# Projecting attention's queries turned and unnormed, with row factors inside the scores' maximum

## The chip, the cores and the metric

The kernel runs on one core of one Trainium2 chip. A core has TensorE (PE, matrix products, with its weight loads shown apart as PEld), VectorE (DVE), ScalarE (ACT), GpSimd (POOL) and SyncE (SP, which here only issues DMAs). Each engine works through its own queue in order and waits on semaphores for the others. The metric is the device time of one execution in microseconds (us); the profile gives, for one such execution, the span from the first to the last instruction.

## The reference, cut to what matters

One encoder layer over two sequences of 512 tokens and width 1024: an S5 state-space branch and a windowed attention branch are gated, added and projected, and a squared-ReLU MLP follows. The change is in attention (16 query heads, 4 key/value heads, head width 64, blocks of 128 tokens, each seeing itself and its neighbours):

```python
h = rms_norm(x, ln1)
q, k, v, u, g_att, g_ssm = jnp.split(h @ w_in, IN_SPLITS, axis=-1)
q = rms_norm(q.reshape(bsz, seq_len, N_HEADS, HEAD_DIM), q_gain)   # per token and head
k = rms_norm(k.reshape(bsz, seq_len, N_KV_HEADS, HEAD_DIM), k_gain)
s = jnp.einsum('nqkgd,njkd->nkgqj', qb, kw) * HEAD_DIM ** -0.5 + bias
s = jnp.where(mask, s, NEG_INF)
p = jax.nn.softmax(jnp.concatenate([s, sink_col], axis=-1), axis=-1)[..., :-1]
o = jnp.einsum('nkgqj,njkd->nqkgd', p, vw)
```

`rms_norm(q)` divides each row (token and head) of the projected queries by the root of its mean square, and multiplies by a gain per column. The divisor is one number per token and head, so it may be applied before or after the product with the keys.

## The kernel before, in words

Products that need full precision are done in three: both operands are split into a high part, rounded by a cast on ACT, and a low rest, subtracted on DVE (or POOL), and high x high, high x low and low x high are added in PSUM.

**The first stage** (0 to some 220 us) projects `u` in eight columns of 128 and the gates in sixteen. The weights of each column come in two DMAs of 256 KB into `c_raw` tiles (two buffers), issued on SP by `column_in` (L212 to L219), are cast on ACT (L222) and split on DVE (L223). The finished columns are stored by SP (`u_store`, L173). Each engine's order is written out by hand here: `fill` holds PE's steps, `cast_owed`, `dve_owed` and `act_owed` what the other engines owe. Column 5 is asked for when column 3's last product is issued; on SP its two loads stand behind three stores of `u` that wait for DVE (L422).

**The attention stage** (436 to some 650 us) has eight steps, one for each key head `j` (0 to 3) and sequence `sq`: `steps = (0,0), (0,1), (1,0), ... (3,1)`. A step has four units `qb`, one for each block of 128 queries, and a unit has four heads. The order on PE, ACT, DVE and POOL is that of the program's text (a manual schedule), so that work of three units lies interleaved:

- the unit itself: `scores` (L1154, PE: high and low keys against the queries), `largest` (L1158, DVE: one custom operation that writes minus (score + bias) to `p` and the minimum to `nmx`), `exp` (L1164, ACT, with the row's sum);
- the unit before (`prev`): its `p` is transposed (L1170), split (L1174 ACT, L1179 DVE) and multiplied with the values (L1186);
- the queries of the next step (`Tile`, four in a step, one in each unit): `project` (L811: 24 products, 128 tokens of `hT` as weights, 256 columns of `w_q` moving), `square` (ACT, L1101), `power` (DVE row sums L1105, POOL L1107 and L1108: x^-0.5), `norm` (DVE, L1112), `turn` (PE, two transposes, L1117), `high` and `low` (two each of 64x256: ACT L1130, DVE L1134) into the tile `qa`.

Keys are copied twice side by side by POOL (`kd`, L1072), transposed (L1081) and split once a step, in the first unit. POOL also multiplies the step's result by its gate and by the softmax's divisors (L1232, L1235), makes the low parts of later query weights (L805), and puts the sink into `p` (L1146). The biases of a key head (128 x 384 for each of its four heads, five buffers) are loaded by SP (L1066) in the last unit before they are needed.

The core of `Tile` and of the maximum, before:

```python
def norm(self):
    self.qn = ap.tile([P, 2, G, HD], F32, tag="qn", name="qn")
    V.tensor_mul(self.qn[:, 0], self.psv, self.rq[:, :, None].to_broadcast([P, G, HD]))

def largest(self, h):
    V.tensor_tensor_reduce(self.p[:, h, 1:1 + self.nk], self.s[h][:, 0:self.nk],
                           biases[self.j][h][:, b0:b0 + self.nk], -1.0,
                           nsink[:, hh:hh + 1], ALU.add, ALU.min, self.nmx[:, h:h + 1])
```

Of the kernel before, what the change touches and what calls it, by code (L numbers as in the profile page):

```python
# [64 lines left out]
def hybrid_layer(ctx, tc, x, xT, rel, onehot, early, w_qkv, w_ug, q_gain, k_gain, sink,  # L65
# [46 lines left out]
    nsink = const.tile([P, N_HEADS], F32, name="nsink")  # L112

# [97 lines left out]

    def column_in(n):  # L212

        src = w_ug[U_BLK + n] if n < KT else w_ug[GA_BLK + n - KT]
        w = weights[n] = [cpool.tile([P, KT, P], F32R, tag=tag, name=tag) for tag in ("c_hi", "c_lo")]
        for i in range(2):
            sl = slice(i * KT // 2, (i + 1) * KT // 2)
            raw = cpool.tile([P, KT // 2, P], F32, tag="c_raw", name="c_raw")
            SP.dma_start(raw, src[:, sl, :])  # L219
# [54 lines left out]
    with tc.tile_pool(name="xin", bufs=2, reuse_waits="tile") as xin, tc.tile_pool(name="ssmc", bufs=1) as sc:  # L274
# [261 lines left out]
        for k in range(KT):  # L536
# [246 lines left out]
    class Block:  # L783
# [24 lines left out]
        def multiply(self, ps, act, col, i0, i1):  # L808
            for i in range(i0, min(i1, 3 * KT)):
                k, p = divmod(i, 3)  # L810
                PE.matmul(ps, act[p == 2][:, k, col:col + P], self.w[k // 4][p == 1][:, k % 4, :],  # L811
                          start=i == 0, stop=i == 3 * KT - 1)
# [240 lines left out]
    with tc.tile_pool(name="att", bufs=2, reuse_waits="tile") as ap:  # L1053
# [32 lines left out]
        class Tile:  # L1086


            def __init__(self, j, sq, t):
                self.key, self.t, self.k, self.qn = (j, sq), t, 0, None  # L1090
# [7 lines left out]
            def square(self):  # L1098
                self.psv = self.ps.rearrange("p (h d) -> p h d", h=G)
                self.sq = ap.tile([P, G, HD], F32, tag="sq", name="sq", bufs=1)  # L1100
                S.activation(self.sq, self.psv, AF.Square, scale=HD ** -0.5)  # L1101

            def power(self):
                ms = small.tile([P, G], F32, tag="ms", name="ms")
                V.reduce_sum(ms, self.sq, axis=AX.X)  # L1105
# [4 lines left out]
            def norm(self):  # L1110
                self.qn = ap.tile([P, 2, G, HD], F32, tag="qn", name="qn")
# [23 lines left out]

        class Unit:


            def __init__(self, j, sq, qb, sums, ya):
                self.j, self.sq, self.qb, self.sums, self.ya = j, sq, qb, sums, ya  # L1140
# [14 lines left out]

            def largest(self, h):
                hh, b0 = self.j * G + h, (self.k0 - self.qb + 1) * P
                V.tensor_tensor_reduce(self.p[:, h, 1:1 + self.nk], self.s[h][:, 0:self.nk],  # L1158
                                       biases[self.j][h][:, b0:b0 + self.nk], -1.0,
# [150 lines left out]
        prev = owed = lower = turned = None  # L1310
# [7 lines left out]
        if True:  # L1318
            rows = entry()
            for i, (j, sq) in enumerate(steps):  # L1320
# [11 lines left out]
                for qb in range(NB):  # L1332
# [7 lines left out]
                    cur = Unit(j, sq, qb, sums, ya)  # L1340
# [6 lines left out]
                    new = Tile(*nxt, qb) if nxt else None  # L1347
                    project = new.project if new else nop
                    kd = None
                    new_biases = (lambda h: load_biases(nxt[0], h)) if nxt and qb == NB - 1 and sq == 1 else nop  # L1350
                    new_biases(0)
                    cur.scores(0)
                    cur.largest(0)
                    new_biases(1)
# [33 lines left out]
                    if rows and not rows.qn:  # L1388
                        rows.norm()
# [835 lines left out]
```

## Time and profile before

| | us |
|---|---|
| Median of 3 runs (lowest, highest) | 1437.83 (1437.75, 1438.02) |
| The profiled execution's own time | 1437.74 |
| Its span | 1436.0 |
| PE, DVE, ACT, POOL busy in it | 1426.7, 1083.2, 770.0, 161.5 |
| Attention stage, first to last unit's start | 436.1 to 641.0 |

The page's rows name a line, an engine, an operation, what it writes and reads, shapes, a count, and then busy time, the mean length of one in ns, and idle time before them with what ended it. A timeline's rows begin with start and duration in us; rows of equal instructions that follow each other are merged (x4), and a bracket gives the idle time before and what ended it. A matmul's recorded length is longer than its share of the engine, since matmuls are pipelined; its cost is read from start to start. A row of a table of stretches gives the stretch, its length, and the busy time and count of PE, PEld, DVE, ACT and POOL, then the granted clock, the DMA engines' share and GB/s.

### The profile page before, as it was taken

To read this page: it belongs to the slowest core of one execution; us is meant where nothing else is said; L and a number is where in the kernel's file an instruction comes from. 1 tells how busy PE (TensorE), PEld (TensorE's weight loads), DVE (VectorE), ACT (ScalarE), POOL (GpSimd) and SP (SyncE) were. 2 spreads that over 40 slices of the span, in tenths; PEclk is the share of its full clock that TensorE was granted. 3 is DMA by queue.
4 is the path that set the end of the run, shared out by engine and by line. 5 is a ranking of instruction groups with operands and counts; after the bars stand their busy time and mean duration, and the time that the engine had idled before them with its cause. 6 is when DMAs were issued, how large, how long until landed. Compare 5 with 4: busy or idle time off the path is not lost.

```text
span 1436.0 us, 21706 instructions
## 1 busy us (share of the span) xinstructions
PE 1426.7 (99%) x7864; PEld 1220.5 (85%) x7864; DVE 1083.2 (75%) x1869; ACT 770.0 (54%) x1390; POOL 161.5 (11%) x230
## 2 busy tenths in 40 slices
PE   9999999999999999999999999999999999999998
PEld 7788888889999999988888888888888888888887
DVE  8799989984637999987754898777776598575644
ACT  7589862234428998895432455545544444333332
POOL 2000010000313554470001100000000000000000
PEclk9999999999999999999999999999999999999999
DMA  8546467358822443356752334444443984464341
GB/s 310 178 153 186 167 208 270 110 194 289 258 81 67 119 130 100 119 184 236 259 178 90 133 118 162 161 161 161 144 140 120 350 323 137 139 201 146 119 132 59
DMA packets 130823, 243.88 MB, mean 170 GB/s; under 512 B 15723, under 2 KB 58987, under 8 KB 130716
## 3 DMA queue, kind: packets, MB, share of 16 engines
q1 hardware_dynamic: 106428, 187.39, 41.0%
q10 hardware_dynamic: 21888, 46.15, 8.5%
q0 software_dynamic: 2400, 8.95, 1.9%
q8 instruction: 62, 1.02, 0.3%
q14 instruction: 45, 0.37, 0.1%
HBM read 174.25 MB, written 80.77 MB: 178 GB/s over the span
## 4 chain that ended last, share of the span: by engine, by line
PE 86%; DVE 7%; DMA 2%; ACT 2%; issue 1%; SPq 0%; POOL 0%; ACTq 0%; DVEq 0%
PE bank L117 14%; PE bank L116 14%; PE bank L118 14%; PE acc L811 9%; PE acc L142 6%; PE acc L849 5%; PE acc L116 3%; PE acc L118 3%; PE acc L117 3%; PE po L1186 3%; PE sps L1154 2%; PE tps L1170 2%; PE sps L956 2%; PE sps L683 2%; DVE tt L887 2%; DMA c_raw<-in_w_ug_dram 1%
## 5 line engine op out<-in xcount | busy, mean ns | idle before, releaser
L117 PE MATMUL bank<-b_lo,a_hi 128*128 128x512 f32 x440 | 171.4, 390 | 0.0
L118 PE MATMUL bank<-b_hi,a_lo 128*128 128x512 f32 x440 | 171.2, 389 | 0.0
L116 PE MATMUL bank<-b_hi,a_hi 128*128 128x512 f32 x440 | 171.2, 389 | 0.0
L2098 ACT CAST a_hi<-d_a 128x1024 fp32r<-128x1024 f32 x55 | 58.1, 1056 | 179.0 <-PE bank L117 175.5
L2099 DVE TENSOR_TENSOR a_lo<-d_a,a_hi 128x1024 fp32r<-128x1024 f32 x55 | 67.3, 1224 | 98.5 <-ACT a_hi L2098 96.4
L116 PE MATMUL bank<-act,u_hi 128*128 128x512 f32 x256 | 99.6, 389 | 0.0
L117 PE MATMUL bank<-act,u_hi 128*128 128x512 f32 x256 | 99.6, 389 | 0.0
L118 PE MATMUL bank<-act,u_lo 128*128 128x512 f32 x256 | 99.6, 389 | 0.0
L117 PEld LDWEIGHTS bank<-b_lo,a_hi 128*128 128x128 f32 x440 | 82.6, 188 | 17.7 <-DVE b_lo L2099 0.6
L116 PEld LDWEIGHTS bank<-b_hi,a_hi 128*128 128x128 f32 x440 | 82.6, 188 | 17.2
L118 PEld LDWEIGHTS bank<-b_hi,a_lo 128*128 128x128 f32 x440 | 82.6, 188 | 16.9
L811 PE MATMUL acc<-w_hi,hT 128*128 128x256 f32 x384 | 84.4, 293 | 0.0
L811 PE MATMUL acc<-w_hi,act 128*128 128x256 f32 x384 | 81.2, 290 | 0.0
L142 PE MATMUL acc<-act,c_hi 128*128 128x512 f32 x256 | 80.8, 395 | 0.0
L142 PE MATMUL acc<-hT,c_hi 128*128 128x512 f32 x256 | 80.8, 395 | 0.0
L1164 ACT ACTIVATE p<-p,nmx 128x257 f32<-128x257 f32 (+1 forms) x128 | 72.1, 564 | 13.0 <-DVE nmx L1158 12.3
L1158 DVE CUSTOM_DVE_ANT_0 p<-sps,bias,nsink 128x256 f32<-128x256 f32 (+1 forms) x128 | 69.3, 542 | 4.3 <-PE sps L1154 2.9
L1882 ACT CAST u_hi<-s 128x512 fp32r<-128x512 f32 x64 | 39.3, 622 | 59.0 <-PE bank L117 40.3
L2099 DVE TENSOR_TENSOR b_lo<-k,b_hi 128x1024 fp32r<-128x1024 f32 x55 | 67.0, 1219 | 0.0
L811 PEld LDWEIGHTS acc<-w_hi,hT 128*128 128x128 f32 x384 | 63.8, 190 | 0.9
L811 PEld LDWEIGHTS acc<-w_hi,act 128*128 128x128 f32 x384 | 63.1, 190 | 0.8
L1179 DVE TENSOR_TENSOR pl<-tps,ph 128x512 fp32r<-128x512 f32 x80 | 55.0, 687 | 4.5 <-ACT ph L1174 2.7
(417 smaller groups left out, 3906.9 us busy)
## 6 DMA issues: line engine op xcount, KB each, us to landing
d_a<-a_scr SPq DMA_DIRECT2D x55, 512.0 KB
u_raw<-in_w_up_dram SPq DMA_DIRECT2D x32, 512.0 KB
a_scr<-t ACTq DMA_DIRECT2D x64, 256.0 KB
k<-in_w_down_dram SPq DMA_DIRECT2D x32, 512.0 KB
a_scr<-a ACTq DMA_DIRECT2D x48, 256.0 KB
c_raw<-in_w_ug_dram SPq DMA_DIRECT2D x44, 256.0 KB
u_sb<-u_scr SPq DMA_DIRECT2D x64, 128.0 KB
ct_scr<-ctab SPq DMA_DIRECT2D x16, 512.0 KB
```

Source lines behind the costliest of these rows:

```text
L116: PE.matmul(ps, a[0], b[0], start=first, stop=False)
L117: PE.matmul(ps, a[0], b[1], start=False, stop=False)
L118: PE.matmul(ps, a[1], b[0], start=False, stop=last)
L142: PE.matmul(self.ps[s], self.w[p == 2][:, k, :], hT[s][p == 1][:, k, :], start=i % (3 * KT) == 0, stop=i % (3 * KT) == 3 * KT - 1)
L811: PE.matmul(ps, act[p == 2][:, k, col:col + P], self.w[k // 4][p == 1][:, k % 4, :], start=i == 0, stop=i == 3 * KT - 1)
L849: PE.matmul(self.ps[s], w_g[self.m][p == 2][:, k, :], y_part(s, int(p == 1), k), start=k + p == 0, stop=k == KT - 1 and p == 2)
L1158: V.tensor_tensor_reduce(self.p[:, h, 1:1 + self.nk], self.s[h][:, 0:self.nk], biases[self.j][h][:, b0:b0 + self.nk], -1.0, nsink[:, hh:hh ...
L1164: S.activation(p, p, AF.Exp, bias=self.nmx[:, h:h + 1], scale=-1.0, accum_out=self.sums[:, h, self.qb:self.qb + 1])
L1179: V.tensor_sub(pl, self.pt[i], self.hl[i][0].bitcast(F32))
L1186: PE.matmul(self.po, vv, self.hl[i][part], start=i + part == 0, stop=i == self.nkb - 1 and part == 1)
L2098: S.copy(hi, src)
L2099: V.tensor_sub(lo, src, hi.bitcast(F32))
```

## The change

In six of the eight steps (`steps[1:-1]`) the queries come as two `Pair`s of heads instead of four `Tile`s. The weights of two heads (128 columns) are now the stationary operand and 512 tokens of `hT` move, so the product comes out turned (head dimensions on partitions), and needs no transposes; it is split at once, with the gain but without the norm. ACT squares it, and PE multiplies the squares (as weights, 128 tokens at a time) with `pair_ones`, a 128x2 matrix of ones in its two halves, which gives each token's sum of squares for both heads. DVE adds EPS, and POOL makes `minus` = -1/rms and `root` = rms from it. POOL then writes bias x rms into `p` for the unit that comes next (`prepare`), and `largest` reads it from there, with `minus` in place of -1: -(1/rms) x (score + bias x rms) is what stood there before. The pairs' 48 products a step are issued as a stream, five of them ahead. The biases' loads are all issued before the unit's first score. In the first stage, the raw weights of column 5 are asked for some 10 us of program order sooner, ahead of the stores.

```diff
+    pair_ones = const.tile([P, 2], F32, name="pair_ones")
...
+    def column_raws(n):
+        src = w_ug[U_BLK + n] if n < KT else w_ug[GA_BLK + n - KT]
+        raws_in[n] = []
+        for i in range(2):
+            raw = cpool.tile([P, KT // 2, P], F32, tag="c_raw", name="c_raw")
+            SP.dma_start(raw, src[:, i * KT // 2:(i + 1) * KT // 2, :])
...
+            if k == 3:
+                column_raws(5)
...
+        def multiply_turned(self, ps, act, m, i0, i1):
+            for i in range(i0, i1):
+                k, p = divmod(i, 3)
+                PE.matmul(ps, self.w[k // 4][p == 2][:, k % 4, m * P:(m + 1) * P], act[p == 1][:, k, :],
+                          start=i == 0, stop=i == 3 * KT - 1)
...
+            def total(self):
+                self.ss = acc() if self.key == turned_steps[-1] and self.m == 0 else tps()
+                for t in range(NB):
+                    PE.matmul(self.ss[:, 2 * t:2 * t + 2], self.sq[:, t * P:(t + 1) * P], pair_ones, start=True, stop=True)
+
+            def mean(self):
+                V.tensor_scalar_add(self.ms, self.ss[:, 0:2 * NB], EPS)
+
+            def factors(self):
+                GP.tensor_tensor(rq, self.ms, neg_half[:, 0:2 * NB], op=ALU.pow)
+                GP.tensor_tensor(root, self.ms, rq, op=ALU.mult)
+                GP.tensor_scalar_mul(minus, rq, -1.0)
...
+            def prepare(self, m):
+                for h in (2 * m, 2 * m + 1):
+                    GP.tensor_scalar_mul(self.p[:, h, 1:1 + self.nk], self.bias(h), self.factor(h, 1))
+
             def largest(self, h):
-                V.tensor_tensor_reduce(self.p[:, h, 1:1 + self.nk], self.s[h][:, 0:self.nk],
-                                       biases[self.j][h][:, b0:b0 + self.nk], -1.0,
+                V.tensor_tensor_reduce(p, self.s[h][:, 0:self.nk], p if raw else self.bias(h),
+                                       self.factor(h, 0) if raw else -1.0,
                                        nsink[:, hh:hh + 1], ALU.add, ALU.min, self.nmx[:, h:h + 1])
...
+                    project = new.project if new else (lambda n: project_turned(n // 2)) if pairs else nop
+                    if i == 0:
+                        project_turned((3, 2, 0, 0)[qb])
+                    if (j, sq) in turned_steps and qb < NB - 1:
+                        upcoming = Unit(j, sq, qb + 1)
+                        for m in range(2):
+                            upcoming.prepare(m)
...
+                    if pairs and qb > 1:
+                        twin.total()
+                        twin.mean()
+                        twin.factors()
+                        if qb == NB - 1:
+                            upcoming.prepare(1)
```

On SP, in the first stage before (`xc` is a column of x, `u_scr` the store of a finished column of `u`, `c_raw` the weights of columns 4 and then 5):

```order
L219 DMA c_raw<-in_w_ug_dram 128x512 x2
L298 DMA xc<-in_xT_dram 128x512 x2
L173 DMA u_scr_75<-up 128x8x128
L173 DMA u_scr_76<-up 128x8x128
L173 DMA u_scr_77<-up 128x8x128
L219 DMA c_raw<-in_w_ug_dram 128x512 x2
```

and of the change:

```order
L223 DMA c_raw<-in_w_ug_dram 128x512 x2
L311 DMA xc<-in_xT_dram 128x512 x2
L223 DMA c_raw<-in_w_ug_dram 128x512 x2
L177 DMA u_scr_75<-up 128x8x128
L177 DMA u_scr_76<-up 128x8x128
L177 DMA u_scr_77<-up 128x8x128
```

The loads of column 5 moved past three stores.

On POOL, from the last unit of a step into the first two units of the next, before (`ms`, `rq` the queries' norm, `fac` the softmax's divisors, `ga` the gate):

```order
L1107 TENSOR_SCALAR ms<-ms 128x4
L1108 TENSOR_TENSOR rq<-ms,neg_half 128x4
L1235 TENSOR_TENSOR ya<-ya,fac 128x1024
L1146 COPY p<-nsink 128x4
L1107 TENSOR_SCALAR ms<-ms 128x4
L1108 TENSOR_TENSOR rq<-ms,neg_half 128x4
L1072 COPY kd<-kn 128x512
L1146 COPY p<-nsink 128x4
```

and of the change (`root` and `minus` the row factors, `p<-bias,root` a prepared bias):

```order
L1315 TENSOR_TENSOR ya<-ya,fac 128x1024
L1213 COPY p<-nsink 128x4
L1233 TENSOR_SCALAR p<-bias,root 128x256 x2
L1185 TENSOR_TENSOR rq_5532<-ms_5530,neg_half 128x8
L1186 TENSOR_TENSOR root<-ms_5530,rq_5532 128x8
L1187 TENSOR_SCALAR minus<-rq_5532 128x8
L1233 TENSOR_SCALAR p<-bias,root 128x256 x2
L1213 COPY p<-nsink 128x4
L1233 TENSOR_SCALAR p<-bias,root 128x384 x4
L1093 COPY kd<-kn 128x512
```

Between the last factors and `kd` there now stand six prepared biases and a copy.

On PE, around the end of a step before (`acc<-w` a query projection, `tps<-ident,p` transposes, `po` products with values, `sps` scores):

```order
L1117 MATMUL acc<-ident,qn 128x128 x2
L1186 MATMUL po<-ph,va 128x512
L811 MATMUL acc<-w_hi,act_113 128x256
L811 MATMUL acc<-w_lo,act_113 128x256
L811 MATMUL acc<-w_hi,act_114 128x256
L811 MATMUL acc<-w_hi,act_113 128x256
L1186 MATMUL po<-pl,va 128x512
L811 MATMUL acc<-w_lo,act_113 128x256
L811 MATMUL acc<-w_hi,act_114 128x256
L1186 MATMUL po<-ph,va 128x512
L1186 MATMUL po<-pl,va 128x512
L1154 MATMUL sps<-kh,qa 128x256
```

and of the change (`squares` the squared pair):

```order
L1266 MATMUL po<-ph,va 128x512
L832 MATMUL acc<-hT_0_120,w_lo 128x512
L832 MATMUL acc<-hT_0_120,w_hi 128x512
L1176 MATMUL tps<-pair_ones,squares 128x2 x4
L1266 MATMUL po<-pl,va 128x512
L832 MATMUL acc<-hT_1_121,w_hi 128x512
L1266 MATMUL po<-ph,va 128x512
L1266 MATMUL po<-pl,va 128x512
L1221 MATMUL sps<-kh,qa 128x256
```

The two transposes of `qn` are gone, six products of 256 columns became three of 512, and four products with `pair_ones` came in, on whose result POOL's row of factors waits.

More of the change, by code (lines that the diff above doesn't have):

```diff
@@ L112, in hybrid_layer @@
     nsink = const.tile([P, N_HEADS], F32, name="nsink")
+    pair_ones = const.tile([P, 2], F32, name="pair_ones")
+    for e in range(2):
+        GP.memset(pair_ones[:, e:e + 1], 0.0)
+        GP.memset(pair_ones[e * 64:e * 64 + 64, e:e + 1], 1.0)
     def mm3(ps, a, b, first, last):
@@ L1309, in hybrid_layer, with project_turned @@
         pending = []
-        prev = owed = lower = turned = None
+        prev = owed = lower = turned = upcoming = twin = None
+        turned_steps, scales, finished = steps[1:-1], {}, []
+        stream = [(key, m) for key in turned_steps for m in range(2)]
+        def project_turned(n):
+            while n and (stream or going):
+                if not going:
+                    going.append(Pair(*stream.pop(0)))
+                n -= going[0].project(n)
+                if going[0].k == 3 * KT:
+                    finished.append(going.pop())
+        going = []
         y_rows, made = [], None
@@ L1346, in hybrid_layer @@
                     div = made if qb == 1 else None
[L1347 to L1348 removed]
+                    new = Tile(*nxt, qb) if nxt and not pairs else None
+                    project = new.project if new else (lambda n: project_turned(n // 2)) if pairs else nop
[5 more added lines that the diff above has]
+                            upcoming.prepare(m)
                     kd = None
                     new_biases = (lambda h: load_biases(nxt[0], h)) if nxt and qb == NB - 1 and sq == 1 else nop
[L1351 removed]
+                    for h in range(G):
+                        new_biases(h)
                     cur.scores(0)
                     cur.largest(0)
[L1354 to L1355 removed]
+                    if rows and not rows.normed:
                         rows.power()
@@ L1387, in hybrid_layer @@
                     cur.exp(1)
-                    if rows and not rows.qn:
+                    if rows and not rows.normed:
                         rows.norm()
@@ L1446, in hybrid_layer @@
                     key_high()
+                    if pairs and qb == NB - 1:
+                        for e in range(2):
+                            twin.high(e)
                     if n3 > 2:
@@ L1456, in hybrid_layer @@
                     turned = rows
+                    if pairs and qb == 2:
+                        for e in range(2):
+                            twin.low(e)
                     project(4)
+                    if pairs and qb > 1:
[4 more added lines that the diff above has]
+                            upcoming.prepare(1)
                     if last:
@@ L1467, in hybrid_layer @@
                         new.square()
+                    if pairs and qb == 1:
+                        twin = finished.pop()
+                        for e in range(2):
+                            twin.high(e)
+                    if pairs and qb == NB - 1:
+                        twin.low(0)
                     if n3:
```

75 lines of the change are left out of this document (59 added, 16 removed).

## The prediction

> **What bounds the kernel now.** I read the page's totals first, then the chain of waits, then a table of busy times for single steps of the attention stage, because the change lies almost wholly there.
>
> ```profile
> span 1436.0 us, 21706 instructions
> PE 1426.7 (99%) x7864; PEld 1220.5 (85%) x7864; DVE 1083.2 (75%) x1869; ACT 770.0 (54%) x1390; POOL 161.5 (11%) x230
> PE 86%; DVE 7%; DMA 2%; ACT 2%; issue 1%; SPq 0%; POOL 0%; ACTq 0%; DVEq 0%
> 514.72:541.35 26.63, 26.63 (x203) 25.38 (x201) 25.04 (x69) 24.26 (x63) 13.45 (x17) 1.00 0.47 123
> ```
>
> TensorE is busy 99% of the span. The last row is one attention step: 26.63 us long, PE busy for all of it at clock 1.00, DVE 25.04 and ACT 24.26 close behind, POOL 13.45. So in this stage a microsecond of PE work saved is a microsecond gained, and relief on DVE or ACT alone is worth nothing.
>
> PE's own idle time is small. The one wait that the change addresses is in the first stage:
>
> ```profile
> 59.59 6.08 DMA c_raw<-in_w_ug_dram
> 59.80 0.59 ACT L236 COPY up<-acc 128x512 f32<-128x512 f32 x1
> 65.75 1.21 ACT L222 CAST c_hi<-c_raw 128x512 fp32r<-128x512 f32 x2 [5.36 <-DMA c_raw<-in_w_ug_dram]
> 64.20 0.39 PE L117 MATMUL acc<-act,c_hi 128*128 128x512 f32 x1
> 64.43 0.39 PE L118 MATMUL acc<-act,c_lo 128*128 128x512 f32 x1
> 66.42 0.50 PE L116 MATMUL acc<-act,c_hi 128*128 128x512 f32 x1 [1.59 <-ACT c_hi L222]
> 66.75 0.40 PE L117 MATMUL acc<-act,c_hi 128*128 128x512 f32 x1
> 67.14 0.50 PE L118 MATMUL acc<-act,c_lo 128*128 128x512 f32 x1
> 67.48 0.39 PE L116 MATMUL acc<-act,c_hi 128*128 128x512 f32 x1
> ```
>
> These are the chain, ACT and PE around 65 us; columns are start, duration, engine, line. The weights of column 5 land at 65.67, ACT casts them, and PE, which starts a 512-wide product every 0.23 us (64.20 to 64.43), loses 66.42 - 64.43 - 0.23 = 1.76 us. The next three starts are 0.33, 0.39 and 0.34 apart, another 0.38 us.
>
> **Part one: the load sooner.** The two DMAs of column 5 move ahead of three stores of `u` on SP's queue. Their buffers held column 4:
>
> ```profile
> 46.01 0.12 DVE c_lo L223
> 61.35 0.22 DVE L581 TENSOR_TENSOR fi<-fi,den 128x64 f32<-128x64 f32 x1
> 66.39 1.29 DVE L223 TENSOR_TENSOR c_lo<-c_raw,c_hi 128x512 fp32r<-128x512 f32 x2 [4.82 <-ACT c_hi L222]
> ```
>
> DVE begins to read column 4's buffers at about 46, so a load of 6.08 us issued at 48 lands by 55. ACT is free at 60.4 (its row at 59.80), so the cast ends by 61.6, and DVE, free at 61.57, has both halves of `c_lo` by 62.9; PE wants them from 64.66. The whole 1.76 + 0.38 = 2.1 us can go. The three `u` stores queue behind two issues that no longer wait. I take -2.0 us, with 0 as the other end (a later wait may take it back).
>
> **Part two: PE in the six steps.** The prices come from a stretch of one step, PE and then its weight loads (PEld), and from two pieces of the chain of waits, a run of 256-wide products (L811) and one of 512-wide (L142):
>
> ```profile
> 510.10 0.60 PE L1170 MATMUL tps<-ident,p 128*128 128x128 f32 x4
> 510.46 0.48 PE L811 MATMUL acc<-w_hi,hT 128*128 128x256 f32 x2
> 510.78 0.28 PE L811 MATMUL acc<-w_lo,hT 128*128 128x256 f32 x1
> 511.01 0.40 PE L1186 MATMUL po<-ph,va 128*128 128x512 f32 x1
> 511.25 0.28 PE L811 MATMUL acc<-w_hi,hT 128*128 128x256 f32 x1
> 510.00 0.46 PEld L1170 LDWEIGHTS tps<-ident,p 128*128 128x128 f32 x4
> 510.43 0.30 PEld L811 LDWEIGHTS acc<-w_hi,hT 128*128 128x128 f32 x2
> 357.66 1.43 PE acc L811 x12
> 196.55 26.79 PE acc L142 x117
> ```
>
> A 256-wide product costs 1.43 / 12 = 0.119 us, a 512-wide one 26.79 / 117 = 0.229, or 0.24 among mixed work (511.01 to 511.25). Four transposes and two products take 510.10 to 510.78 = 0.68, so a transpose costs (0.68 - 0.24) / 4 = 0.11.
>
> - Projection: 96 products 128x256 a step become 48 of 128x512 with the same columns: 96 x 0.119 = 11.42 against 48 x 0.229 = 10.99. That is -0.43 a step, -2.6 in six; at 0.24 apiece it would be +0.1 a step.
> - The 8 transposes of normed queries a step go: 8 x 0.11, -0.88 a step, -5.3 in six.
> - New: the row sums of squares, 8 products a step of a full 128x128 fp32 weight (`squares`) with two columns. No row shows that shape. The trace runs a plain fp32 product twice: the sixteen of the lag row below are eight in the program. So 16 passes a step. Each brings its own weight load. The rows show an exposed load: the first L811 pair after the transposes lasts 0.48 (510.46) though its two starts are otherwise 0.12 apart, because its load could only begin at 510.43, and the last transpose started then; two loads from 510.43 to 510.66 (0.30 less the 0.19 of one record) are 0.11 apart. With two columns nothing covers the load, so I take 0.11 a pass: 16 x 0.11 = 1.76 a step, +10.6 in six. The other end is the shortest pace in the trace, with 32-column weights:
>
> ```profile
> 180.59 0.65 PE L696 MATMUL lag<-ctab,lbt 128*32 128x128 f32 x16
> 181.17 0.50 PE L142 MATMUL acc<-hT,c_hi 128*128 128x512 f32 x1
> ```
>
> (181.17 - 180.59) / 16 = 0.036 a pass, 3.5 us for 96 passes.
>
> PE's sum is -2.6 - 5.3 + 10.6 = +2.7 us: the new sums cost more than the transposes and the narrow products that they replace.
>
> **Part three: DVE and ACT.** They get shorter, not longer:
>
> ```profile
> L1134 DVE SCALAR_TENSOR_TENSOR qa<-acc,gain_q,qa 64x256 fp32r<-64x256 f32 x33 | 16.0, 484 | 0.8
> L1105 DVE TENSOR_REDUCE ms<-sq 128x4 f32<-128x256 f32 x16 | 6.7, 417 | 0.5
> L1112 DVE TENSOR_TENSOR qn<-acc,rq 128x256 f32<-128x256 f32 x16 | 6.6, 414 | 0.0
> L1084 DVE SCALAR_TENSOR_TENSOR kl<-tps,gain_k,kh 128x512 fp32r<-128x512 f32 x4 | 3.0, 751 | 0.9 <-ACT kh L1083 0.9
> L1207 DVE RECIPROCAL rsum<-sm 128x16 f32<-128x16 f32 x4 | 1.0, 241 | 0.0
> ```
>
> In these four steps the three lines that go cost DVE (16.0 + 6.7 + 6.6) / 4 = 7.3 us a step. In their place come four `low` of 64x512 (0.75 as `kl`, up to 2 x 0.484) and two `mean` (0.16 between nothing and the 0.24 of L1207): 3.3 to 4.2. DVE falls to about 22 of 26.6 us, and ACT's fewer, wider operations fall too. I cost this at nothing, since PE is the bound; the maxima only swap -1 for a factor per row, and cost nothing either. POOL's four `pair_ones` fills stand at the program's start, where it sits idle for 12.88 us. SP's bias loads change place:
>
> ```profile
> 15.21 0.22 POOL L390 TENSOR_SCALAR ss<-ss 128x1 f32<-128x1 f32 x1 [12.88 <-ACT rn_junk L388]
> 477.56 6.98 SPq L1066 DMA_DIRECT2D bias<-line_scr  x3
> 487.15 0.42 SPq L1066 DMA_DIRECT2D bias<-line_scr  x1
> ```
>
> Three used to go in one row and the fourth 9 us after the first; now the four go together, ahead of a store. POOL reads them in the middle of a step's last unit, DVE used to in the next step's first. POOL's own preparations free their buffers a unit sooner than the maxima did, so I cost this at nothing; a load that lands late would lengthen part four.
>
> **Part four: POOL at the step boundary.** POOL now scales the biases, 16 operations a step, in a queue with all else. The last pair's row sums are made near the end of a step, and behind them stand, in order: power, root, minus, two preparations 128x256, a copy, four preparations 128x384 for the next unit, and `kd`, for whose transposes PE waits in the next step's first unit.
>
> ```profile
> 542.70 0.23 POOL L1107 TENSOR_SCALAR ms<-ms 128x4 f32<-128x4 f32 x1 [2.66 <-DVE ms L1105]
> 543.01 1.04 POOL L1108 TENSOR_TENSOR rq<-ms,neg_half 128x4 f32<-128x4 f32 x1
> 544.01 0.61 POOL L1072 COPY kd<-kn 128x512 f32<-128x512 f32 x1
> 544.56 0.19 POOL L1146 COPY p<-nsink 128x4 f32<-128x4 f32 x1
> 552.92 1.30 POOL L805 TENSOR_TENSOR w_lo<-w_raw,w_hi 128x512 fp32r<-128x512 f32 x1
> ```
>
> A hand-over costs 0.08 (542.93 to 543.01). From the start of the last sum: its result 0.28, `mean` 0.16, power 1.04, root 0.25 (between 0.23 and 1.04), minus 0.23, the small copy 0.19, `kd` 0.61, five hand-overs 0.40: 3.16. The six preparations are unseen: priced as copies (0.19 at 4 columns, 0.61 at 512) they are 2 x 0.40 + 4 x 0.50 = 2.8; as two-input operations (1.30 at 512) 2 x 0.65 + 4 x 0.98 = 5.2. They read one tensor, so I take the copies: 6.0 us. PE meanwhile walks from the last sum to `kd`: one pass 0.11, fifteen 512-wide products 3.44, eight of 256 0.95 and eight transposes 0.88: 5.4. POOL's operations overlap by some 0.06 each (544.56 against 544.62), which may take 0.3 off its 6.0. Of what is left, 0.3 to 0.6, I take 0.5 of PE waiting at each boundary, +3.0 in six; the ends are 0 and, at the two-input price, 8.4 - 0.1 - 5.4 = 2.9 each.
>
> **Sum.** -2.0 + 2.7 + 3.0 = +3.7 us on the profiled execution's 1437.74, which is 0.09 below the median of 1437.83: 1441.4 us.
>
> **Rivals.** (1) *The sums cost their two columns, not their weight loads*: 96 x 0.036 = 3.5 for 10.6, so 1441.4 - 7.1 = 1434.3, faster. For it: they are tiny. Against it: the exposed load at 510.43, and DVE and ACT, 22 to 24 us in each step and waiting on one another, which stand close behind PE. The Trainium skill, "TensorE: Matmul & The Clock Gate", Back-to-back issue gap, gives about 60 cycles for 1 to 64 columns; by that (25 ns) the sum would be 8.2 lower. The same page, LDWEIGHTS, lets a load take its columns over 1.2 GHz, 107 ns for 128, and there the trace agrees with 0.11.
> (2) *POOL is in time*: the preparations come out 0.1 shorter each, `kd` is no longer late, and 1441.4 - 3.0 = 1438.4 is no change. For it: POOL has half its time free. The Trainium skill, "GPSIMD Engine Reference", Engine selection, calls one-input operations roughly line-rate; at its 1.2 GHz that is 0.32 for 384 columns, and by it, as an estimate, PE would not wait; no run here shows it yet.
> (3) *POOL becomes the bound*: at the two-input price each boundary is 2.9 late, 17.4 for 3.0, and the time 1455.8. It decides from about 0.7 us for 384 columns, where six boundaries cost some 8 us.
> (4) *The load goes out no sooner*, its buffers still held: +2.0, 1443.4.
>
> **How the numbers follow.** The forecast has 0.43, rival 1 0.15, rival 2 0.28, rival 3 0.09, rival 4 0.05. The range reaches from just under rival 1 to half-way to rival 3: 1433.0 to 1448.0; the forecast's own is 1439 to 1444.5. A measurement here tells 0.2% (2.9 us) from no change: below 1434.9 counts as faster, above 1440.7 as slower. The forecast straddles the upper mark, 0.29 slower and 0.14 same; rival 1 gives 0.11 faster and 0.04 same, rival 2 0.25 same and 0.03 faster, rivals 3 and 4 are slower. Together 0.14, 0.43 and 0.43.
>
> **What would show it.** The wait at 66 us gone; a 512-wide turned product every 0.23 us; the sums' passes 0.11 apart (0.04 for rival 1); 128x384 preparations of 0.5 us (0.3 for rival 2, near 1 for rival 3); a PE wait before the `kd` transposes in the first unit; DVE at 22 us a step; steps of 27.0 to 27.5 us instead of 26.6. I am wrong if steps get shorter than 26.6, or if a wait that I cost at nothing, of ACT or DVE, sets their length.

## The result, and the profile after

The change made the kernel slower: 1499.34 us (median; 1497.39 to 1499.68) against 1437.99 (1437.75 to 1438.37), a ratio of 1.0425 [1.0414, 1.0437]. The forecast was 1441.4 with a range up to 1448.0. The profiled execution took 1499.45 us, its span is 1497.6.

The page of the changed kernel: the span, the engines' busy time, the shares of the chain that ended last, and the group of POOL's preparations.

```profile
span 1497.6 us, 21301 instructions
...
PE 1460.9 (98%) x7624; PEld 1217.5 (81%) x7624; DVE 1072.3 (72%) x1809; ACT 760.8 (51%) x1354; POOL 257.4 (17%) x318
...
PE 91%; POOL 4%; ACT 2%; issue 1%; DVE 1%; DMA 1%; SPq 0%; ACTq 0%; POOLq 0%; DVEq 0%
...
L1233 POOL TENSOR_SCALAR p<-bias,root 128x256 f32<-128x256 f32 (+1 forms) x96 | 102.5, 1086 | 0.0
```

PE is busy 34 us longer than before although it has fewer products, and POOL, which had 0% of the chain, now has 4%. Two separate places account for this. The first is the attention stage; the table of busy times for one step (columns as before: stretch, length, PE, PEld, DVE, ACT, POOL, granted clock):

```profile
533.27:567.83 34.56, 29.80 (x162) 24.95 (x161) 22.86 (x59) 22.93 (x56) 29.46 (x32) 0.90 0.34 101
```

The step takes 34.56 us instead of 26.63. POOL works 29.46 of it (13.45 before), DVE has fallen to 22.86 as forecast, and the clock is 0.90. At the boundary between two steps, POOL's timeline and what PE waited for in five steps (total, times, longest, in us):

```profile
567.98 1.67 POOL L1185 TENSOR_TENSOR rq<-ms,neg_half 128x8 f32<-128x8 f32 x1
569.72 0.20 POOL L1186 TENSOR_TENSOR root<-ms,rq 128x8 f32<-128x8 f32 x1
569.90 0.24 POOL L1187 TENSOR_SCALAR minus<-rq 128x8 f32<-128x8 f32 x1
570.12 1.82 POOL L1233 TENSOR_SCALAR p<-bias,root 128x256 f32<-128x256 f32 x2
571.89 0.19 POOL L1213 COPY p<-nsink 128x4 f32<-128x4 f32 x1
572.05 4.90 POOL L1233 TENSOR_SCALAR p<-bias,root 128x384 f32<-128x384 f32 x4
576.89 0.61 POOL L1093 COPY kd<-kn 128x512 f32<-128x512 f32 x1
```

```profile
PE tps L1102 <- POOL kd L1093: 21.7, 5, 4.6
```

This is the queue that the prediction's part four listed, in its order, and PE waits for `kd` as it said. The sizes differ: a preparation of 384 columns takes 1.23 us where 0.50 was taken, the power 1.67 where 1.04 was, and PE stands up to 4.6 us where 0.5 was forecast.

The second place lies outside attention. A run of 512-wide products in the first stage, from the chain of waits, which before read "196.55 26.79 PE acc L142 x117", 0.229 us apiece:

```profile
195.16 27.50 PE acc L146 x117
```

The same 117 products now take 27.50, 0.235 apiece, at clock 1.00. Nothing in the diff touches them.

### The profile page after: what moved, and what is told of

It reads as the page before. It is cut to its first block, busy times and chain, and to the rows that moved or that the text cites. A ratio compares the mean times of both kernels' runs of the same rounds, so it can differ in the third digit from the quotient of the medians.

```text
span 1497.6 us, 21301 instructions
## 1 busy us (share of the span) xinstructions
PE 1460.9 (98%) x7624; PEld 1217.5 (81%) x7624; DVE 1072.3 (72%) x1809; ACT 760.8 (51%) x1354; POOL 257.4 (17%) x318
## 4 chain that ended last, share of the span: by engine, by line
PE 91%; POOL 4%; ACT 2%; issue 1%; DVE 1%; DMA 1%; SPq 0%; ACTq 0%; POOLq 0%; DVEq 0%
PE bank L122 13%; PE bank L120 13%; PE bank L121 13%; PE acc L146 11%; PE acc L870 5%; PE acc L832 4%; PE acc L826 4%; PE acc L120 3%; PE acc L122 3%; PE acc L121 3%; POOL p L1233 3%; PE po L1266 2%; PE sps L1221 2%; PE sps L977 2%; PE sps L698 2%; PE tps L1250 2%
## 5 line engine op out<-in xcount | busy, mean ns | idle before, releaser
L1233 POOL TENSOR_SCALAR p<-bias,root 128x256 f32<-128x256 f32 (+1 forms) x96 | 102.5, 1086 | 0.0
L121 PE MATMUL bank<-act,u_hi 128*128 128x512 f32 x256 | 101.3, 396 | 0.0
L120 PE MATMUL bank<-act,u_hi 128*128 128x512 f32 x256 | 101.2, 396 | 0.0
L1238 DVE CUSTOM_DVE_ANT_0 p<-sps,p,nsink 128x256 f32<-128x256 f32 (+1 forms) x96 | 57.9, 603 | 17.3 <-PE sps L1221 11.6
L122 PEld LDWEIGHTS bank<-act,u_lo 128*128 128x128 f32 x256 | 48.1, 188 | 11.7
L120 PEld LDWEIGHTS bank<-act,u_hi 128*128 128x128 f32 x256 | 48.1, 188 | 11.6
L121 PEld LDWEIGHTS bank<-act,u_hi 128*128 128x128 f32 x256 | 48.1, 188 | 11.6
```

What stands on the lines that cost most here:

```text
L120: PE.matmul(ps, a[0], b[0], start=first, stop=False)
L121: PE.matmul(ps, a[0], b[1], start=False, stop=False)
L122: PE.matmul(ps, a[1], b[0], start=False, stop=last)
L1233: GP.tensor_scalar_mul(self.p[:, h, 1:1 + self.nk], self.bias(h), self.factor(h, 1))
L1238: V.tensor_tensor_reduce(p, self.s[h][:, 0:self.nk], p if raw else self.bias(h), self.factor(h, 0) if raw else -1.0, nsink[:, hh:hh + 1], ...
```

## The experiments

Times are medians beside runs of the kernel before on the same chip (1437.5 to 1438.0 each time). Theories A to C are those of the expectation printed above each result.

### The load alone

The kernel before, with `raws_in`, `column_raws` and its call at `k == 3` taken over from the change, and nothing else.

> The kernel before with the first stage's edit alone: the raw weights of column 5 asked for ahead of the three stores of u. The prediction's part one: PE's wait of 1.76 us at 66.42 us and the three late starts behind it go, -2.0 us, 1436.0 us (1435.7 to 1436.4). Its rival 4, that the buffers are still held: 1438.0 us.

Measured: 1434.42 us, ratio 0.9979 [0.9969, 0.9988], some 3 us faster than before. PE's timeline at the place of the wait:

```profile
64.66 0.39 PE L118 MATMUL acc<-act,c_lo 128*128 128x512 f32 x1
64.88 0.39 PE L116 MATMUL acc<-act,c_hi 128*128 128x512 f32 x1
```

The product that started at 66.42 starts at 64.88, 0.22 after the one ahead of it. Part one holds in its mechanism; the gain is 1 us larger than its 2.0, and that part builds up in small steps later and is not explained. This kernel is the fastest of all that were run.

### Where the tiles lie

Four kernels. The tile `pair_ones` has 8 bytes in each partition, and since tiles in this program begin at multiples of 32 bytes, the tiles that are placed behind it move by 32.

```diff
 # the kernel before, and this, read by nobody (moves by 32 bytes)
+    pair_ones = const.tile([P, 2], F32, name="pair_ones")
...
 # the change, moved by 64; the third kernel has 32 columns (128 bytes)
-    pair_ones = const.tile([P, 2], F32, name="pair_ones")
+    pair_ones = const.tile([P, 16], F32, name="pair_ones")
...
 # the change, nothing moved
-    pair_ones = const.tile([P, 2], F32, name="pair_ones")
+    pair_ones = neg_half[:, 14:16]
```

> The kernel before with nothing but the tile pair_ones (128 x 2, filled by POOL, read by nobody) added behind nsink, so that every tile that is placed after it lies 32 bytes further on, as in the change. Theory A (layout): the place of the tiles sets the pace of the 512-wide products. Outside attention the change's products start every 233.5 ns where before they start every 227 ns, which there adds about 2.8 us between 208 and 306 us and 11.4 us between 650 and 1118 us, while the 256-wide products fall from 120 to 117 ns (1 to 3 us less). Then this kernel takes 1448 to 1452 us. Theory B (something that the changed attention stage leaves behind, or POOL's heavier work, slows the products): this kernel has the old attention stage and takes 1438.0 us, within 0.5, with products every 227 ns.

> The change with pair_ones 16 columns wide instead of 2, of which only the first two are filled and read; the tiles behind it lie 64 bytes further on than in the kernel before, instead of 32. Theory A (layout): the 512-wide products are back at 227 ns, the 256-wide ones at 120; the time falls by 11 to 16 us to 1483 to 1488 us, and the steps of attention are shorter by some 0.3 us (48 turned products x 6.5 ns) but keep POOL's wait. Theory B (the changed attention stage or POOL's work slows the later products): no change, 1499.3 us within 1.

> The change with pair_ones 32 columns wide (128 bytes), of which two are filled and read: the tiles behind it lie 128 bytes further on than in the kernel before. A move by 32 bytes took the products from 227 to 233.5 ns, and a move by 64 left them there. Theory A (the pace hangs on where weights and moving operand lie to one another modulo 128 bytes): products at 227 ns again outside attention, 256-wide ones at 120, 1484 to 1488 us; POOL's waits in attention stay. Theory B (something else in the kernel, not the place, keeps them slow): 1498 us, as with 64 bytes.

> The change with one edit: pair_ones lies in two unused columns of the tile neg_half, so that no tile outside attention moves against the kernel before; the four fills remain. Theory A (the place of the tiles): 512-wide products at 227 ns outside attention, 1484 to 1488 us with attention's waits as they are. Theory B (the fills, or the changed attention stage, slow them): 233 ns and 1497 to 1499 us.

Measured: 1450.50 us, ratio 1.0088 [1.0072, 1.0103], for the old kernel with an unused tile; 1497.95 (1.0416 [1.0402, 1.0431]) for the change moved by 64 bytes, 1497.32 (1.0413 [1.0399, 1.0427]) by 128, and 1484.26 (1.0321 [1.0307, 1.0335]) with nothing moved. The run of 117 products in these four, in that order, and in the run with single sums and shared work below, where the tiles lie 256 bytes further on:

```profile
196.72 27.50 PE acc L146 x117
```

```profile
195.06 27.50 PE acc L146 x117
```

```profile
194.82 27.37 PE acc L146 x117
```

```profile
194.19 26.79 PE acc L146 x117
```

```profile
194.26 26.79 PE acc L148 x117
```

An unused tile of 8 bytes costs the old kernel 13 us, and taking the move back, with the four fills kept, gives the change 15.1 us, so the place does it and not the fills. The first theory of a period (64, then 128 bytes) was wrong: 27.50, 27.50, 27.37 for 32, 64 and 128 bytes, and 26.79 for 0 and 256. The moving operand of these 117 products (`hT`) lies in tiles at the other end of the memory, which did not move, while the weights did. Whether the distance between the two counts or the weights' place by itself was not told apart.

### `kd` ahead of the preparations

```diff
+                    kd = key_copies(*nxt) if qb == 0 and nxt else None
                     if (j, sq) in turned_steps and qb < NB - 1:
                         upcoming = Unit(j, sq, qb + 1)
...
-                    if qb == 0 and nxt:
-                        kd = key_copies(*nxt)
```

> The change with one move on POOL: the copy kd goes ahead of the four preparations 128x384 of the next unit, which take 4.9 us in the change's rows. Theory A (place in the queue): PE waits for kd only because of what stands ahead of it; each of the six waits of 4.6 us before the kd transposes goes and nothing takes its place, the steps fall from 34.5 us to 28.6 to 29.2, and the time to 1463 to 1468 us. Theory B (POOL is the bound): POOL is busy 29.4 us of a step; with kd early the wait moves to the maxima, which then wait for the preparations, and a step cannot be shorter than POOL's 29.4 us: steps of 29.6 to 31, time 1469 to 1478 us, and DVE rather than PE is the engine that waits for POOL.

Measured: 1473.48 us, ratio 1.0247 [1.0233, 1.0261]; 26 us of the loss go. A step, and the waits of PE for `kd` and of DVE's maxima for the preparations:

```profile
551.34:580.79 29.45, 28.16 (x163) 23.49 (x161) 22.92 (x58) 22.86 (x56) 29.29 (x32) 1.00 0.24 73
```

```profile
PE tps L1102 <- POOL kd L1093: 2.7, 3, 1.0
```

```profile
DVE p L1238 <- POOL p L1233: 3.4, 6, 1.6
```

POOL is busy 29.29 of 29.45 us: the place in the queue made part of the wait, but with `kd` early POOL itself sets the step. That is theory B.

### What POOL is paid for

One kernel prepares each head of a unit in its own way:

```diff
-                    GP.tensor_scalar_mul(self.p[:, h, 1:1 + self.nk], self.bias(h), self.factor(h, 1))
+                    p, bias, root = self.p[:, h, 1:1 + self.nk], self.bias(h), self.factor(h, 1)
+                    if h == 0:
+                        GP.tensor_copy(p, bias)
+                    elif h == 1:
+                        GP.tensor_scalar_mul(p, bias, 1.0)
+                    elif h == 2:
+                        GP.tensor_scalar_mul(p, bias, root)
+                    else:
+                        GP.tensor_tensor(p, bias, root.to_broadcast([P, self.nk]), op=ALU.mult)
```

> The change with POOL's preparation done in four ways, one for each head of a unit: head 0 a plain copy of the bias and head 1 a product with the constant 1.0 (both leave out the factor rms), head 2 the product with the row factor as in the change, head 3 a two-input product with the factor broadcast along the row. Theory A (POOL pays for the kind of operation): the copy stays near the prediction's price, 0.5 us for 384 columns, and the products take about 1 us or more. Theory B (the factor read from a column of its own makes it dear): copy and constant both near 0.5 us, the row factor 1.24, the broadcast 1.0. Theory C (reading the bias or writing the strided rows of p makes it dear): all four 1.0 us or more. Where two of four are cheap, POOL has some 5 us less in a step and most of PE's wait for kd goes.

Measured in one run: 1478.93 us. POOL's groups, then PE's wait for `kd`:

```profile
L1239 POOL TENSOR_SCALAR p<-bias,root 128x384 f32<-128x384 f32 x12 | 15.0, 1246 | 0.0
...
L1237 POOL TENSOR_SCALAR p<-bias 128x384 f32<-128x384 f32 x12 | 14.1, 1172 | 0.0
...
L1241 POOL TENSOR_TENSOR p<-bias,root 128x384 f32<-128x384 f32 x12 | 9.9, 828 | 0.0
...
L1241 POOL TENSOR_TENSOR p<-bias,root 128x256 f32<-128x256 f32 x12 | 7.4, 618 | 0.0
...
L1235 POOL COPY p<-bias 128x384 f32<-128x384 f32 x12 | 6.1, 507 | 0.0
```

```profile
PE tps L1102 <- POOL kd L1093: 13.5, 6, 2.3
```

The copy costs 0.507 us, the prediction's 0.50. A product with one number costs 1.17 to 1.25, and the two-input product with a broadcast factor 0.83: it is the kind of operation that is dear (theory A), and the one-input form is the dearest. With less work ahead of `kd` the wait shrinks, from 4.6 to 2.3 us at the longest.

### The work shared out

POOL keeps heads 0 and 1, ACT prepares head 2, DVE head 3; `kd` first; tiles moved by 128 bytes. The second kernel adds single-pass row sums and lies at 256 bytes.

```diff
+            def prepare_late(self, h):
+                p = self.p[:, h, 1:1 + self.nk]
+                if h == 2:
+                    S.activation(p, self.bias(h), AF.Copy, scale=self.factor(h, 1))
+                else:
+                    V.tensor_scalar_mul(p, self.bias(h), self.factor(h, 1))
...
 # the second kernel also
-                self.sq = ap.tile([P, HALF], F32, tag="qn", name="squares")
+                self.sq = ap.tile([P, HALF], F32R, tag="qn", name="squares")
```

> The change with pair_ones 128 bytes wide, kd ahead of the next unit's preparations, and the preparations shared out: heads 0 and 1 stay on POOL, head 2 goes to ACT ahead of the unit's first exponential, head 3 to DVE ahead of its third maximum. POOL's 29.4 us a step fall by 8 x 1.09 = 8.7 to about 21; ACT and DVE get four operations of about 0.5 us each, to about 25. Theory A (POOL was the whole of the loss in attention, the layout the whole of it outside): PE sets the pace again with steps of 26.6 + 0.45 = 27.0 us, and the time is 1438.0 - 3.0 (the load alone) + 2.7 (the prediction's sum for PE) = 1437.7, between 1436 and 1440. Theory B (the maxima now wait for ACT's and DVE's extra work, one after the other): steps of 28 us or more and 1443 us or more.

> As the run with the shared preparations, and the squares and the ones rounded to the type of the split operands (fp32r), so that a row sum is one pass over PE instead of two: 48 passes in six steps instead of 96. Theory A (each pass costs its weight load, 0.112 us): 48 x 0.112 = 5.4 us less than that run, 1432 if it takes 1437.7. Theory B (PE no longer sets the step): the same time as that run. The sums of squares are less exact by the rounding of each square.

Measured: 1488.04 us, ratio 1.0347 [1.0333, 1.0361], and 1473.18, 1.0243 [1.0229, 1.0257]. A step of the first kernel:

```profile
530.30:563.84 33.54, 29.88 (x162) 23.65 (x161) 27.25 (x63) 24.82 (x61) 21.94 (x24) 0.98 0.38 107
```

POOL's work fell to 21.94 us as reckoned, yet the step takes 33.5: theory B, and by far more than the four operations that it named, with DVE at 27.25. DVE's and ACT's groups of the new preparation over four steps, and rows of DVE and POOL:

```profile
L1241 DVE TENSOR_SCALAR p<-bias,root 128x256 f32<-128x256 f32 (+1 forms) x16 | 18.3, 1141 | 0.0
```

```profile
L1239 ACT ACTIVATE p<-bias,root 128x256 f32<-128x256 f32 (+1 forms) x16 | 9.0, 565 | 0.1
```

```profile
534.71 0.51 DVE L1241 TENSOR_SCALAR p<-bias,root 128x256 f32<-128x256 f32 x1
...
557.07 2.39 POOL L1323 TENSOR_TENSOR ya<-ya,fac 128x1024 f32<-128x1024 f32 x1
...
557.24 2.36 DVE L1241 TENSOR_SCALAR p<-bias,root 128x256 f32<-128x256 f32 x1
...
549.32 0.41 DVE L1241 TENSOR_SCALAR p<-bias,root 128x384 f32<-128x384 f32 x1
```

ACT does it in 0.57 us. DVE takes 256 columns once in 0.51 and once in 2.36, where it ends 0.14 after a POOL operation that began just before it; its mean is 1.14. With POOL idle beside it, which happened to four of the sixteen, even 384 columns take only 0.41 (last row). So about (18.3 - 16 x 0.41) / 4 = 2.9 us of DVE's step are spent behind POOL, as an estimate; what else the 33.5 consist of was not taken apart. The Trainium skill, "SBUF — State Buffer", Who interferes with whom, says that `tensor_scalar` on DVE can enter a mode that takes the pair of ports shared with GpSimd, and that whichever comes second is blocked for the whole instruction; these rows agree. The difference between the two kernels, 14.9 us, is mostly the layout (13.1 for 128 bytes: 1497.32 - 1484.26), so some 2 us are left for the sums.

### POOL made shorter, in place

The change with `pair_ones` in `neg_half`, `kd` and the preparations behind the row factors of the queries, and the cheapest form that still multiplies. The second kernel adds single-pass sums at 256 bytes.

```diff
-                    GP.tensor_scalar_mul(self.p[:, h, 1:1 + self.nk], self.bias(h), self.factor(h, 1))
+                    GP.tensor_tensor(self.p[:, h, 1:1 + self.nk], self.bias(h),
+                                     self.factor(h, 1).to_broadcast([P, self.nk]), op=ALU.mult)
```

> The change with three edits: pair_ones lies in two unused columns of the tile neg_half, so that no tile moves; kd and the next unit's preparations stand behind the row factors of the queries on POOL, kd first; and the preparations are two-input products with the factor broadcast along the row, which took 0.83 us for 384 columns and 0.62 for 256 where the product with a row factor took 1.25 and 0.93. POOL's work falls from 29.4 us a step by 16 x 1.09 - 8 x 0.83 - 8 x 0.62 = 5.8 to about 23.6. Theory A (POOL's time was the loss in attention, the layout the loss outside it): PE sets the pace with steps of 27.0 to 27.3 us at clock 1.00 and the time is 1438.0 - 3.0 (the load alone) + 2.7 (the prediction's sum for PE) = 1437.7, between 1436 and 1440. Theory B (the order on POOL still makes PE wait at the step's boundary, or DVE, whose maxima read what POOL has just written, becomes late): steps of 28 us or more, 1443 us or more.

> As the run with POOL's work made shorter, but pair_ones 256 bytes further on in tiles of its own, and squares and ones rounded to fp32r, so that each row sum is one pass over PE: 48 passes in six steps instead of 96. Theory A (each pass costs its weight load of 0.112 us and PE sets the pace): 5.4 us less, 1432.3 us if that run takes 1437.7, and faster than the kernel before by 5 to 6 us. Theory B (PE does not set the pace): no difference to that run. Layout: 256 bytes leave the 512-wide products at 227 ns, as the last such run had them.

Measured: 1447.95 us, ratio 1.0069 [1.0055, 1.0082], and 1448.72, 1.0077 [1.0063, 1.0091]. One step of each:

```profile
517.51:545.92 28.41, 28.18 (x162) 23.57 (x161) 22.75 (x58) 22.84 (x56) 23.27 (x32) 1.00 0.42 122
```

```profile
517.40:545.84 28.44, 28.01 (x155) 22.51 (x154) 22.66 (x58) 22.95 (x57) 23.30 (x33) 1.00 0.42 122
```

POOL no longer sets the step, the clock is 1.00, and against the change with nothing moved 36.3 us are gone (1484.26 to 1447.95). But the step takes 28.4 us, not 27.0, and it takes 28.4 also when PE has eight passes fewer: PE does not set it. Theory B of both.

### What sets the rest

Four kernels, all from the one with single-pass sums. The first two change the order of the last pair's split (on ACT and DVE, and on DVE alone), the others what the maxima read.

```diff
 # DVE alone: the low parts of the last pair
                     cur.largest(1)
                     if twin and qb == 0:
-                        twin.low(1)
-                        twin = None
+                        twin.low(0)
...
                         prev.low(0)
+                    if twin and qb == 0:
+                        twin.low(1)
+                        twin = None
...
-                    if pairs and qb == NB - 1:
-                        twin.low(0)
...
 # the maxima with a constant
-                                       self.factor(h, 0) if raw else -1.0,
+                                       -1.0,
...
 # the maxima with the bias
-                V.tensor_tensor_reduce(p, self.s[h][:, 0:self.nk], p if raw else self.bias(h),
+                V.tensor_tensor_reduce(p, self.s[h][:, 0:self.nk], self.bias(h),
```

> As the run with single-pass row sums, with the last pair's split moved on ACT and DVE: of its two halves only the first is copied high in the step's last unit; its low part goes behind the second maximum of the next step's first unit, and the second half's high and low parts go behind that unit's first transposes. In that run the steps took 28.4 us, as long as with two-pass sums, and DVE stood 1.02 us waiting for ACT's copies of these halves with the first maximum of the next step queued behind it. Theory A (this order on DVE and ACT sets the length of the step now): steps of 27.0 to 27.8 us, time 1441 to 1446 us. Theory B (the wait is hidden; some other chain sets the step): 28.4 us and 1448.7 us, within 1.

> As the run with single-pass row sums, with DVE's order alone changed at the step's boundary: the low part of the last pair's first half stands behind the second maximum of the next unit, and that of its second half behind the low part of that unit's first transposes; ACT's copies stay where they were. In that run DVE stood 1.02 us at the boundary, waiting for ACT's copies, with the first maximum behind. Theory A (that place on DVE sets the length of the step): the wait goes and steps take 27.4 to 28.0 us, 1444 to 1447 us. Theory B (the queries' low parts are then late for the third and fourth scores, as in the run that moved ACT's copies too): PE waits there instead, 28.4 us or more, 1448 to 1452 us.

> As the run with single-pass row sums, and the maxima take the constant -1 again in place of the factor per row (this leaves the division of the scores by rms out; the bias is still multiplied by rms). In the change each maximum took 62 ns more than before, 0.96 us of DVE in a step. Theory A (reading the factor per row costs the 62 ns, and DVE sets the step): maxima of 480 and 604 ns, steps of 27.5 to 28.0 us instead of 28.4, time 1444 to 1447 us. Theory B (the 62 ns come from reading p in place of the bias): maxima stay at 540 and 662 ns, same time. Theory C (the factor costs the 62 ns, but DVE is not what sets the step): shorter maxima, same steps and 1448.7 us.

> As the run with single-pass row sums, and the maxima read the bias itself, as before the change, with the factor per row kept (this leaves the multiplication of the bias by rms out of the result; POOL still makes it). Theory A of the run with the constant: maxima stay at 540 and 662 ns. Theory B: they fall to 480 and 604 ns.

Measured: 1451.72 us, ratio 1.0099 [1.0082, 1.0115], with ACT and DVE reordered; 1450.61, 1.0085 [1.0069, 1.0102], with DVE alone; 1445.30, 1.0047 [1.0033, 1.0062], with the constant; 1449.11 in one run with the bias. DVE's wait for ACT's copies in the kernel that the four start from, PE's wait with DVE alone reordered, then the maxima of the change, with the constant, and with the bias (there one group holds 48 maxima with the factor and 16 with the constant):

```profile
DVE qa L1203 <- ACT qa L1199: 5.1, 5, 1.0
```

```profile
PE sps L1223 <- DVE qa L1203: 7.5, 5, 1.7
```

```profile
L1238 DVE CUSTOM_DVE_ANT_0 p<-sps,p,nsink 128x384 f32<-128x384 f32 x48 | 32.0, 666 | 16.5 <-PE sps L1221 11.6 <-POOL p L1233 4.5
L1238 DVE CUSTOM_DVE_ANT_0 p<-sps,p,nsink 128x256 f32<-128x256 f32 x48 | 25.9, 541 | 0.8
```

```profile
L1241 DVE CUSTOM_DVE_ANT_0 p<-sps,p,nsink 128x384 f32<-128x384 f32 x48 | 28.9, 602 | 8.5 <-PE sps L1223 6.7 <-POOL p L1235 1.4
L1241 DVE CUSTOM_DVE_ANT_0 p<-sps,p,nsink 128x256 f32<-128x256 f32 x48 | 23.0, 479 | 0.8
```

```profile
L1241 DVE CUSTOM_DVE_ANT_0 p<-sps,bias,nsink 128x256 f32<-128x256 f32 x64 | 33.5, 525 | 1.9 <-PE sps L1223 0.8
```

A factor per row makes a maximum 62 ns longer, whichever tensor is read beside it: (48 x 541 + 16 x 480) / 64 = 526 is what the last row shows. Taking it away gives 3.4 us (1448.72 to 1445.30): DVE's maxima are on the path. The split at the boundary has a wait at either end: done early, DVE waits for ACT's copies with the next step's first maximum queued behind (5.1 us in five steps); done later, PE waits for the queries (7.5 us in five steps). That the early place costs time is not shown, since neither move made the kernel faster. With the constant a step still takes 27.8 us:

```profile
516.00:543.79 27.79, 27.44 (x154) 22.53 (x153) 21.72 (x58) 22.91 (x57) 23.32 (x32) 1.00 0.43 125
```

No engine but PE is near that length, and PE's 27.44 holds its short waits for the others. What sets the 27.8 us stays open, and how much of it the boundary is worth: no order that avoids both waits was found.

## Why the prediction was wrong

Of the 57.9 us between forecast and result, 15.1 are the layout, some 33 POOL (36.3 measured, 3.0 forecast), and 9.5 the rest (1447.95 with the layout mended and POOL's work shortened, against 1441.4 - 3.0 = 1438.4 without POOL's term). Of the rest, 3.4 are the factor in the maxima; for the other 6 no run shows the cause.

- **The load sooner (-2.0)** was right in its mechanism: the wait at 66.42 is gone. By itself it gave some -3, a third of which is unexplained.
- **PE's sum (+2.7)** had its prices right. The eight passes of one pair's row sums (four products, two passes each) in the changed kernel, between their neighbours on PE's timeline:

```profile
523.82 0.39 PE L832 MATMUL acc<-hT,w_hi 128*128 128x512 f32 x1
524.05 0.98 PE L1176 MATMUL tps<-pair_ones,squares 128*128 128x2 f32 x8
524.89 0.48 PE L1266 MATMUL po<-pl,va 128*128 128x512 f32 x1
```

(524.89 - 524.05) / 8 = 0.105 a pass, 0.11 forecast; rival 1 (0.036) is out. PE was not what set the step any more, though, so the sum did not decide: with half the passes the step stayed at 28.4 us.
- **Part three, "I cost this at nothing, since PE is the bound", failed.** DVE fell to 22.9 us, close to the forecast 22, but the maxima were said to "only swap -1 for a factor per row, and cost nothing either". They cost 16 x 0.062 = 1.0 us a step, and of these 6 us in six steps the time showed 3.4. Low busy time was taken for slack, in a stage where DVE and ACT wait on one another.
- **Part four, the preparations priced as copies, failed, and it is the main step.** "They read one tensor, so I take the copies", it said. Reading one tensor did not decide the price: 1.25 us for 384 columns, where the copy takes 0.51. The order of the queue and the wait for `kd` were right. With the measured prices the prediction's own working even gives the wait: 0.28 + 0.16 and two hand-overs of 0.08 to the power's start, 576.89 + 0.61 - 567.98 = 9.52 from there to the end of `kd`, 10.1 in all; less PE's 5.4 that is 4.7. But that is luck in part, since two errors cancel:

```profile
565.99 0.95 PE L1176 MATMUL tps<-pair_ones,squares 128*128 128x2 f32 x8
566.80 0.48 PE L1266 MATMUL po<-pl,va 128*128 128x512 f32 x1
572.40 0.63 PE L832 MATMUL acc<-hT,w_hi 128*128 128x512 f32 x2
577.56 0.69 PE L1102 MATMUL tps<-ident,kd 128*128 128x128 f32 x2 [4.53 <-POOL kd L1093]
566.19 1.83 POOL L1233 TENSOR_SCALAR p<-bias,root 128x256 f32<-128x256 f32 x2
```

The last pass starts at about 566.70, yet the power not 0.6 but 1.28 us later, because POOL is still at two preparations that stood ahead of it in the queue (566.19 + 1.83 = 568.02). So POOL needs 577.50 - 566.70 = 10.8 us. PE in turn is at work until 572.40 + 0.63 = 573.03, or 6.3 us instead of 5.4, and 10.8 - 6.3 = 4.5. The sentence of the Trainium skill that rival 2 weighed, "GPSIMD Engine Reference", Engine selection, one-input operations roughly line-rate, holds for the copy at best; for the product the trace is against it.
- **Rival 3, POOL as the bound (0.09)**, is what happened, and its point, 0.7 us for 384 columns, was passed. Its price, 17.4 us, was too small for four reasons: the two-input price that served as the upper end (0.98) was below the measured one-input price; the power of eight columns took 0.63 more than that of four; PE's clock was halved behind each of the six waits, as the last section shows; and POOL was counted at the boundary alone, never over a step. There the sixteen preparations take 16 x 1.09 = 17.4 us instead of the 8 x 0.40 + 8 x 0.50 = 7.2 of the forecast's prices, and POOL's 29.46 us are more than the 26.63 of the old step: that is why moving `kd` ahead could not bring the old step back.
- **The layout was in no part.** "POOL's four `pair_ones` fills" were costed, the eight bytes that they fill were not. 512-wide products outside attention went from 0.229 to 0.235 us.

## What to carry to other kernels

Price an operation on POOL by a row of the same operation: a copy and a product with one number, of the same shape, differed by a factor of 2.3 to 2.5. When that engine then holds more work than the step is long, moving one instruction in its queue does not bring the old time back (the move of `kd` took off 26 of the 61 us, and the step stayed at POOL's length). A new small tile is part of the change: place it where nothing moves (an unused column of another tile), and compare start-to-start times of products that the diff doesn't touch before looking for the loss in those that it does. Take parts of a change singly, since here one of them alone (the load) beat both kernels.

## What the runs showed of the hardware

- **The place of tiles.** With the moving operand in place, a 512-wide product whose weights lie 32, 64 or 128 bytes further on takes 0.234 to 0.235 us instead of 0.229, at 256 bytes 0.229 again. Other distances were not tried.
- **The clock after a wait.** The stretch after PE's wait of 4.5 us in the changed kernel, then two stretches of the kernel with four prices, after waits of 2.3 and of 2.0 us:

```profile
543.00:546.50 3.50, 3.48 (x11) 3.00 (x12) 0.75 (x1) 1.26 (x3) 3.50 (x4) 0.50 0.00 0
```

```profile
534.10:537.50 3.40, 3.32 (x20) 2.99 (x21) 1.76 (x4) 2.14 (x4) 3.40 (x6) 1.00 0.00 0
```

```profile
471.30:474.70 3.40, 3.40 (x11) 2.91 (x12) 0.75 (x1) 1.32 (x3) 3.40 (x5) 0.53 0.21 66
```

After the longest wait the granted clock is 0.50 for 3.5 us, which is 1.75 us of PE work lost in a step. After the wait of 2.3 us it stays at 1.00, but after the shorter one, of 1.96 us, it is 0.53; so the length of a wait alone does not decide here. In the first kernel with shared work the clock was 0.50 from 562.70 to 565.50 us, after a wait of 1.71 us that ended at 561.24. The Trainium skill, "TensorE: Matmul & The Clock Gate", What's actually happening, puts the gate at an idle window of about 3.4 us; the first two rows fit a wait of that length as the limit, the third does not. What else decides was not tested.
- **DVE behind POOL.** A DVE product of 256 columns with one factor lasted until just after POOL's operation had ended, 2.36 us, where 384 columns with POOL idle took 0.41.
- **A power on POOL** took 1.67 us for 8 columns and 1.04 for 4, so doubling the columns added 0.63.
